# Hybrid mixer block on one core: splitting, transposing and gating the projection's results while it runs, memory tokens in plain fp32, half of a branch projection within retention

## The chip, the cores and the metric

The kernel runs on one core of one Trainium2 chip. The metric is the time of one execution in microseconds (us); of several runs the median is taken. The engines are TensorE (PE in the rows, with its weight loads as PEld), VectorE (DVE), ScalarE (ACT), GpSimd (POOL) and SyncE (SP), which issues nearly all DMAs here. TensorE's clock is granted at one of two levels, 1.2 and 2.4 GHz; the rows give the mean as a share of the higher one.

## The reference

One decoder layer over 1024 rows of 1024 features. `z` is 13312 columns wide and is cut into the operands of three branches and three gates.

```python
h = rms_norm(x, g_mix[l])
z = h @ w_in[l]
rq, rk, rv, rg, dq, dk, dv, cq, gates = split_cols(z, SPLITS)
ret = retention_chunkwise(rq, rk, rv)              # 4 heads, chunks of 128 rows
ret = jax.nn.swish(rg) * head_norm(ret, g_ret[l], True)
y_ret = ret @ w_ret_o[l]                           # 2048 -> 1024
da = diff_attention(dq, dk, dv, lam)               # 4 heads, causal, ALiBi
y_diff = head_norm(da, g_diff[l], False) * (1.0 - lam_init) @ w_diff_o[l]
kv = rms_norm(mem, g_mem[l]) @ w_mem_kv[l]         # 256 memory tokens
ca = memory_cross_attention(cq, mk, mv)
y_cross = ca.reshape(b, s, CROSS_W) @ w_cross_o[l]
g = jax.nn.sigmoid(gates)
merged = g[0] * y_ret + g[1] * y_diff + g[2] * y_cross
x = x + merged @ w_out[l]
u = jax.nn.relu(rms_norm(x, g_ffn[l]) @ w_up[l])
x = rms_norm(x + (u * u) @ w_down[l], g_final)
```

## The kernel before, in words

Features lie on the 128 partitions and rows of the sequence along the free axis, in two halves `t` of 512. Nearly every product is three matmuls (`mm3`, L144 to L146): each operand is split into a high and a low fp32r part, and high x high, high x low and low x high are added in PSUM. A split is a cast on ScalarE (L131) and a subtraction on VectorE (L132). The stages follow each other:

1. **Prologue.** `x` is normalized and made into the seven operands `hop` of a seven-product scheme. Beside that the keys and values of the memory tokens are computed (`mem_keys`, `mem_values`): 16 weight tiles `kst`, each split into `kw`, against the split memory `mh`, in 384 matmuls of 256 columns.
2. **Projection.** 52 units of 256 columns of `z` go through `seven`: seven `quad`s of twelve 512-column matmuls each, with the left operands (`wo`) made by ScalarE and VectorE one unit ahead. `z_emit` is called four times in a unit (tile `zo`): VectorE adds a PSUM tile and an earlier copy `s`, or ScalarE copies, and SP stores the fp32 tile to DRAM. The units run in the order cq, dq, dk, dv, rk, rq, rv, rg, gates.
3. **Cross-attention**, 4. **differential attention**: `load_halves` loads a tile of `z` (`raw`), and ScalarE and VectorE split it; `dv` is transposed on TensorE first (`dvt`). After every second block, `fill` puts one half tile of a branch's output projection (`branch_halves`, 24 matmuls `y`) between.
5. **Retention**, 32 steps (4 heads x 8 chunks). `ret_prepare` forms the scores from plain fp32 operands (`rsc`, L784), and transposes and splits v and k (`rvt`, `rkt`); `ret_product` multiplies and updates the state; `ret_store` transposes the result (`rot`) and stores it (`rn`). 16 `fill`s of the second branch's projection lie in every second step.
6. **Retention's output projection** (`branch`, w_ro in two halves of 8 features blocks): `make_ret` loads `rn` and `rg`, multiplies by the gate on ScalarE, VectorE and GpSimd, and splits (`ar`), twice; then 384 matmuls `y` each time.
7. Output projection (`wo`), MLP and the final norm.

Gates are loaded and put through a sigmoid beside each `y` tile (L454, L944). Instructions reach each engine's queue in an order that a scheduler fixes when the program is built; each engine then works through its own queue in that order.

Of the kernel before, what the change touches and what calls it, by code (L numbers as in the profile page):

```python
# [18 lines left out]
P = 128  # L19
# [16 lines left out]
FILL_R = [[1, 0] * 4] * 4  # L36
# [21 lines left out]
def hybrid_block(  # L58
# [57 lines left out]
    z_d = pairs("z", NU)  # L116
# [6 lines left out]
    def z_of(col, t):  # L123
        return z_d[INDEX[col]][t]

    def gate_of(n, t):
        return z_of(GT + (n // 2) * 256, t)[:, n % 2]
# [69 lines left out]
    def left_operands(pool, src0, src1):  # L197
# [10 lines left out]
        for key, src in (  # L208
            ("11", ra[:, 0]), ("12", ra[:, 1]), ("2", s2), ("1", s1), ("3", rb[:, 0]), ("22", rb[:, 1]), ("4", s4)
        ):  # L210
            w = pool.tile([P, 2, HALF], F32R, tag="wo", name="wo", bufs=12)
            split(w[:, 0], w[:, 1], src)
            ops[key] = w
# [16 lines left out]
    def seven(units, ops, load, tmp, emit):  # L230
# [3 lines left out]
        def begin(u):  # L234
# [3 lines left out]
            s1 = tmp.tile([P, HALF], F32, tag="s1", name="s1", bufs=2)  # L238
# [5 lines left out]
        for i, u in enumerate(units):  # L244
# [13 lines left out]
            s3 = tmp.tile([P, HALF], F32, tag="s3", name="s3", bufs=2)  # L258
# [17 lines left out]
    def kv_load(src):  # L276
        st = sp0.tile([P, 1024], F32, tag="kst", name="kst", bufs=3)
        nc.sync.dma_start(out=st, in_=src)
        return st

    def kv_split(st):
        w = sp0.tile([P, 2, 1024], F32R, tag="kw", name="kw", bufs=2)
        split(w[:, 0], w[:, 1], st)
        return w
# [6 lines left out]
    early = [kv_load(w_kv[f]) for f in range(2)]  # L291
# [24 lines left out]
    mh = [sp0.tile([P, 2, HALF], F32R, name=f"mh{j}", tag=f"mh{j}") for j in range(4)]  # L316

    def mem_hl(k):
        v = mh[k // 2]
        c = (k % 2) * NMEM  # L320
        return v[:, 0, c : c + NMEM], v[:, 1, c : c + NMEM]

    for j in range(4):
        r = sp0.tile([P, HALF], F32, tag="tt", name="mr", bufs=6)
        for k in (2 * j, 2 * j + 1):
            c = (k % 2) * NMEM
            src = mt[k // 4][:, (k % 4) * NMEM : (k % 4 + 1) * NMEM]
            scale_rows(r[:, c : c + NMEM], src, vec[:, V_MEM + k : V_MEM + k + 1], rb[:, :NMEM])
        split(mh[j][:, 0], mh[j][:, 1], r)
# [5 lines left out]
    def x_steps():  # L335
        for t in range(2):
            for acc in wide_sums([xr[kp][t].rearrange("p a c -> p (a c)") for kp in range(4)]):
                yield
            rb = rms_finish(acc, HALF)
            yield  # L340
            for kp in range(4):
                for a in range(2):
                    v = xr[kp][t][:, a]
                    k = 4 * a + kp
                    scale_rows(v, v, vec[:, V_MIX + k : V_MIX + k + 1], rb)
# [5 lines left out]
        for kp in range(4):  # L351
# [4 lines left out]
            add(b12, b22, b12, ALU.subtract)  # L356
            add(t4, b21, t2, ALU.subtract)
# [17 lines left out]
    def mem_keys(f):  # L375
        hl = kv_split(early[f] if f < 2 else kv_load(w_kv[f]))
        o = mm_ps("mk")
        for k in range(KT):
            sl = slice(k * P, (k + 1) * P)
            mm3(o[:, :NMEM], (hl[:, 0, sl], hl[:, 1, sl]), mem_hl(k), k == 0, k == KT - 1)  # L380
        kv_store(mk_d[f // 2][:, f % 2], o[:, :NMEM])

    def mem_values(h):
        hls = [kv_split(kv_load(w_kv[8 + 2 * h + j])) for j in range(2)]
        for m in range(2):
            o = mm_ps("mv")
            for k in range(KT):
                c = (k % 4) * 256
                w = hls[k // 4]
                a = tuple(v[:, m * P : (m + 1) * P] for v in mem_hl(k))  # L390
                mm3(o[:, :256], a, (w[:, 0, c : c + 256], w[:, 1, c : c + 256]), k == 0, k == KT - 1)
# [19 lines left out]
    def z_emit(u, n, t, a, b):  # L411
        st = zt.tile([P, HALF], F32, tag="zo", name="zo", bufs=4)
        if b is None:
# [3 lines left out]
        nc.sync.dma_start(out=z_d[u][t][:, n], in_=st)  # L417
# [28 lines left out]
    def branch_halves(b, w, w0, rhs, before):  # L446

        for d in range(8):
            hl = weight(w[w0 + d])
            for t in range(2):  # L450
# [3 lines left out]
                nc.scalar.activation(out=g, in_=g, func=AF.Sigmoid)  # L454
                add(g, o, g, ALU.mult)
                if before:
                    m = zs_tile("hf", "m")
                    nc.sync.dma_start(out=m, in_=mg_d[d][t])
                    nc.gpsimd.tensor_tensor(out=g, in0=g, in1=m, op=ALU.add)
                nc.sync.dma_start(out=mg_d[d][t], in_=g)  # L460
                yield

# [23 lines left out]
    def v_tile(name):  # L486
        return cp.tile([P, 2, 2, 256], F32R, tag="v", name=name, bufs=4)
# [673 lines left out]
```

## Time and profile before

| | us |
|---|---|
| median of 3 runs | 2768.16 (2762.69 to 2782.67) |
| the profiled execution | 2767.48 |
| its span | 2765.7 |
| PE busy | 2610.9 (94%) |
| DVE busy | 1567.6 (57%) |
| ACT busy | 998.0 (36%) |
| POOL busy | 127.2 (5%) |

The span is what the trace covers, and the profiled execution's own time is 1.8 us more. Busy shares are means over the stages listed above, which differ; a stage's share is read from its own stretch. The mean granted clock is 0.975 of the higher level. A matmul's row is longer than its distance to the next one, since matmuls are pipelined; the distance between starts is the price in a stream.

### The profile page before, as it was taken

To read this page: it belongs to the slowest core of one execution; us is meant where nothing else is said; L and a number is where in the kernel's file an instruction comes from. 1 tells how busy PE (TensorE), PEld (TensorE's weight loads), DVE (VectorE), ACT (ScalarE), POOL (GpSimd) and SP (SyncE) were. 2 spreads that over 40 slices of the span, in tenths; PEclk is the share of its full clock that TensorE was granted. 3 is DMA by queue.
4 is the path that set the end of the run, shared out by engine and by line. 5 is a ranking of instruction groups with operands and counts; after the bars stand their busy time and mean duration, and the time that the engine had idled before them with its cause. 6 is when DMAs were issued, how large, how long until landed. Compare 5 with 4: busy or idle time off the path is not lost. (4 is left out here: it accounts for less than half of the span.)

```text
span 2765.7 us, 32055 instructions
## 1 busy us (share of the span) xinstructions
PE 2610.9 (94%) x12126; PEld 2145.0 (78%) x12126; DVE 1567.6 (57%) x2749; ACT 998.0 (36%) x1803; POOL 127.2 (5%) x135
## 2 busy tenths in 40 slices
PE   6899999999999998799879998699999999999998
PEld 5788888888888887688767776477888888888887
DVE  7745454454544542877768787554564444544445
ACT  5433333333333332667665443332342112121222
POOL 0000000000000000000101111320000000000001
PEclk9999999999999999899989999699999999999999
DMA  5333332333333332423327443653321111111111
GB/s 201 135 111 110 114 112 103 111 108 114 114 103 111 107 107 88 157 92 127 121 92 252 159 156 127 212 179 102 123 88 54 46 46 46 46 56 52 46 38 61
DMA packets 135595, 299.15 MB, mean 108 GB/s; under 512 B 13712, under 2 KB 42384, under 8 KB 135440
## 3 DMA queue, kind: packets, MB, share of 16 engines
q1 hardware_dynamic: 135296, 297.06, 31.8%
q8 instruction: 95, 1.56, 0.2%
q14 instruction: 60, 0.49, 0.1%
q10 hardware_dynamic: 144, 0.03, 0.0%
HBM read 215.26 MB, written 81.79 MB: 107 GB/s over the span
## 5 line engine op out<-in xcount | busy, mean ns | idle before, releaser
L144 PE MATMUL x<-hop,wo 128*128 128x512 f32 x1456 | 575.1, 395 | 6.0 <-ACT wo L131 5.3
L146 PE MATMUL x<-hop,wo 128*128 128x512 f32 x1456 | 571.7, 393 | 0.0
L145 PE MATMUL x<-hop,wo 128*128 128x512 f32 x1456 | 566.1, 389 | 0.0
L146 PEld LDWEIGHTS x<-hop,wo 128*128 128x128 f32 x1456 | 274.0, 188 | 64.4 <-DVE wo L132 0.2
L144 PEld LDWEIGHTS x<-hop,wo 128*128 128x128 f32 x1456 | 274.4, 188 | 61.0 <-ACT wo L131 5.5
L145 PEld LDWEIGHTS x<-hop,wo 128*128 128x128 f32 x1456 | 274.0, 188 | 61.3
L132 DVE TENSOR_TENSOR wo<-wr,wo 128x512 fp32r<-128x512 f32 x208 | 143.7, 692 | 238.6 <-ACT wo L131 238.6
L149 DVE TENSOR_TENSOR zo<-x,s 128x512 f32<-128x512 f32 x156 | 107.9, 692 | 243.2 <-PE x L146 127.7
L131 ACT CAST whl<-wst 128x1024 fp32r<-128x1024 f32 x112 | 115.8, 1047 | 336.3 <-PE dn L146 257.3
L1040 DVE TENSOR_TENSOR x<-x,dn 128x512 f32<-128x512 f32 (+1 forms) x248 | 164.5, 669 | 128.0 <-PE dn L146 127.6
L145 PE MATMUL dn<-u,whl 128*128 128x512 f32 (+1 forms) x544 | 207.4, 381 | 0.0
L144 PE MATMUL dn<-u,whl 128*128 128x512 f32 (+1 forms) x544 | 206.4, 379 | 0.0
L146 PE MATMUL dn<-u,whl 128*128 128x512 f32 (+1 forms) x544 | 204.5, 376 | 0.0
L145 PE MATMUL u<-h,whl 128*128 128x512 f32 x512 | 200.4, 391 | 0.0
L144 PE MATMUL u<-h,whl 128*128 128x512 f32 x512 | 199.8, 390 | 0.0
L146 PE MATMUL u<-h,whl 128*128 128x512 f32 x512 | 199.6, 390 | 0.0
L131 ACT CAST wo<-wr 128x512 fp32r<-128x512 f32 x208 | 128.9, 622 | 165.6 <-PE x L146 161.9
L132 DVE TENSOR_TENSOR whl<-wst,whl 128x1024 fp32r<-128x1024 f32 x112 | 143.2, 1289 | 32.7 <-ACT whl L131 32.2
L1018 DVE TENSOR_TENSOR ur<-ur 128x512 f32<-128x512 f32 x64 | 44.3, 692 | 194.9 <-ACT ur L1017 194.9
L144 PE MATMUL y<-ar,whl 128*128 128x512 f32 x256 | 105.8, 416 | 35.5 <-ACT ar L131 35.5
L131 ACT CAST wo<-ws 128x512 fp32r<-128x512 f32 x156 | 96.8, 622 | 110.0 <-PE x L146 106.3
L132 DVE TENSOR_TENSOR wo<-ws,wo 128x512 fp32r<-128x512 f32 x156 | 107.2, 689 | 27.1 <-ACT wo L131 27.0
(243 smaller groups left out, 4680.0 us busy)
## 6 DMA issues: line engine op xcount, KB each, us to landing
wr<-in_w_z SPq DMA_DIRECT2D x104, 512.0 KB, 3.4
z<-zo SPq DMA_DIRECT2D x208, 256.0 KB, 2.0
g<-z SPq DMA_DIRECT2D x64, 256.0 KB, 3.4
wst<-in_w_up SPq DMA_DIRECT2D x32, 512.0 KB, 3.3
wst<-in_w_down SPq DMA_DIRECT2D x32, 512.0 KB, 3.3
raw<-z SPq DMA_DIRECT2D x24, 512.0 KB, 3.3
kst<-in_w_kv SPq DMA_DIRECT2D x16, 512.0 KB, 4.0
mg<-g SPq DMA_DIRECT2D x32, 256.0 KB, 2.0
```

What stands on the lines that cost most here:

```text
L131: nc.scalar.copy(out=hl_hi, in_=src)
L132: eng.tensor_tensor(out=hl_lo, in0=src, in1=hl_hi.bitcast(F32), op=ALU.subtract)
L144: nc.tensor.matmul(out, ah, bh, start=first, stop=False, skip_group_check=again)
L145: nc.tensor.matmul(out, ah, bl, start=False, stop=False, skip_group_check=again)
L146: nc.tensor.matmul(out, al, bh, start=False, stop=last, skip_group_check=again)
L149: nc.vector.tensor_tensor(out=out, in0=a, in1=b, op=op)
L1018: nc.vector.tensor_tensor(out=r, in0=r, in1=r, op=ALU.mult)
L1040: nc.vector.tensor_tensor(out=x2[d][t][:, cols], in0=x2[d][t][:, cols], in1=o[:, :width], op=ALU.add)
```

## The change

The splits, transposes and gates that stages 3 to 6 did after loading `z` are done in `z_emit`, before the store. Query and key tiles are stored as split pairs (`zh`, 512 KB instead of 256 KB for a tile); k and v of retention and v of the differential branch are transposed there (four 128x128 transposes, tile `zt`, for each of the 64 tiles of 16 units) and stored split (`zth`, also in tag `zh`, two buffers). `rg` becomes swish times the gain, the gates become sigmoids. The later stages load them ready. Retention's scores take the split pairs, as six fp32r matmuls of 128 columns instead of two plain fp32 ones. In the prologue the memory products are 128 plain fp32 matmuls, without splits; half of the scaling of `x` and two of its four subtractions go to ScalarE and GpSimd. `FILL_R` puts a half tile into every retention step: first the 16 of w_do, then from step h = 2, c = 1 the first half of w_ro, whose features are by then stored. The second half of w_ro runs after retention. GpSimd's add in `branch_halves` goes to VectorE, and two scalings of results (`don`, `on`) go from VectorE to ScalarE.

```diff
-FILL_R = [[1, 0] * 4] * 4
+FILL_R = [[1] * 8] * 4
...
     def mem_keys(f):
-        hl = kv_split(early[f] if f < 2 else kv_load(w_kv[f]))
+        w = early[f] if f < 4 else kv_load(w_kv[f])
         o = mm_ps("mk")
         for k in range(KT):
-            sl = slice(k * P, (k + 1) * P)
-            mm3(o[:, :NMEM], (hl[:, 0, sl], hl[:, 1, sl]), mem_hl(k), k == 0, k == KT - 1)
+            nc.tensor.matmul(
+                o[:, :NMEM], w[:, k * P : (k + 1) * P], mem_of(k), start=k == 0, stop=k == KT - 1
+            )
...
     def z_emit(u, n, t, a, b):
+        col = ORDER[u]
         st = zt.tile([P, HALF], F32, tag="zo", name="zo", bufs=4)
+        if col >= GT:
+            if b is not None:
+                add(st, a, b)
+            nc.scalar.activation(out=st, in_=a if b is None else st, func=AF.Sigmoid)
+            nc.sync.dma_start(out=z_d[col][t][:, n], in_=st)
+            return
         if b is None:
             nc.scalar.copy(out=st, in_=a)
         else:
             add(st, a, b)
-        nc.sync.dma_start(out=z_d[u][t][:, n], in_=st)
...
+        if col in zh_d:
+            zh = zt.tile([P, 2, HALF], F32R, tag="zh", name="zh", bufs=2)
...
+                split(zh[:, 0], zh[:, 1], st)
+            nc.sync.dma_start(out=zh_d[col][t][:, :, n], in_=zh.bitcast(F32))
+        if col in zt_d:
+            tp = sc_ps("zt")
+            for i in range(4):
+                nc.tensor.transpose(out=tp[:, i * P : (i + 1) * P], in_=st[:, i * P : (i + 1) * P], identity=ident)
+            zh = zt.tile([P, 2, HALF], F32R, tag="zh", name="zth", bufs=2)
...
+                split(zh[:, 0], zh[:, 1], tp)
+            nc.sync.dma_start(
+                out=zt_d[col][t][:, :, :, n * P : (n + 1) * P],
+                in_=zh.rearrange("p a (i c) -> p a i c", i=4).bitcast(F32),
+            )
...
     def cross_probs(h, mk, t):
-        q = load_halves(qk_tile("q", "cq"), z_of(CQ + h * 256, t))
+        q = load(qk_tile("q", "cq"), zh_d[CQ + h * 256][t])
...
-    def ret_prepare(h, c, kqv):
...
+    def ret_prepare(h, c, kq):
...
         for d in range(2):
-            nc.tensor.matmul(sp[:, :P], kc[:, d], qc[:, d], start=d == 0, stop=d == 1)
+            mm3(sp[:, :P], (k[:, 0, d, sl], k[:, 1, d, sl]), (q[:, 0, d, sl], q[:, 1, d, sl]), d == 0, d == 1)
...
+        vhl = rp.tile([P, 2, HALF], F32R, tag="vhl", name="vhl", bufs=3)
+        for b in range(2):
+            nc.sync.dma_start(
+                out=vhl[:, :, b * 256 : (b + 1) * 256].bitcast(F32), in_=zt_d[RV + h * 512 + b * 256][t][:, :, i]
+            )
...
+            if h == 2 and c == 1:
+                drain()
+                ar = [[None] * 2 for _ in range(KT)]
+                for t in range(2):
+                    ret_features(0, 4, t)
+                halves = branch_halves(0, w_ro, 0, hl_rhs(ar), True)
             fill(FILL_R[h][c])
...
+    for t in range(2):
+        ret_features(4, 8, t)
+    halves = branch_halves(0, w_ro, 8, hl_rhs(ar), True, out=mg)
+    drain()
...
-    branch(2, 0, w_ro, 0, make_ret(0))
-    branch(3, 0, w_ro, 8, make_ret(4))
```

`ret_features`, new, loads a stored feature tile into `arr` (tag `hf`, two buffers of the pool) and splits it into `ar`, whose memory is that of the operand tiles of the branch projected before.

TensorE's queue in the projection, at the seam between one unit's last product (`x3`) and the next unit's first (`x2`), in a unit of dv. Before:

```order
L145 MATMUL x3_3044<-hop_1001,wo_2874 128x512
L146 MATMUL x3_3044<-hop_1001,wo_2874 128x512
L144 MATMUL x2_3151<-hop_430,wo_2996 128x512
L145 MATMUL x2_3151<-hop_430,wo_2996 128x512
L146 MATMUL x2_3151<-hop_430,wo_2996 128x512
```

The same seam now:

```order
L156 MATMUL x3_3133<-hop_705,wo_2923 128x512
L154 MATMUL x2_3264<-hop_374,wo_3077 128x512
L155 MATMUL x2_3264<-hop_374,wo_3077 128x512
L156 MATMUL x2_3264<-hop_374,wo_3077 128x512
L154 MATMUL x2_3264<-hop_395,wo_3077 128x512
L449 MATMUL zt_3223<-ident_68,zo_3221 128x128 x4
L155 MATMUL x2_3264<-hop_395,wo_3077 128x512
```

The transposes of a tile stand four matmuls (elsewhere seven) behind the product that it came from, in the middle of the next one.

ScalarE's queue over most of one unit of rk (`s` are the copies that free `x1` for TensorE's next product, `wo` the operands of the next unit). Before:

```order
L131 CAST wo<-ws 128x512 [waits DVE_49,PE_49]
L254 COPY s_3453<-x_3348 128x512 [waits PE_49]
L131 CAST wo<-wr 128x512 [waits DMAHW7_49]
L131 CAST wo<-wr 128x512 [waits PE_49]
L259 COPY s_3480<-x_3348 128x512 [waits PE_49]
L131 CAST wo<-ws 128x512 [waits DVE_49,Activation_49]
L239 COPY s_3498<-x_3485 128x512 [waits PE_49]
L131 CAST wo<-ws 128x512 [waits Activation_49]
L414 COPY zo<-x_3348 128x512 [waits DMAHW7_49,PE_49,Activation_49]
```

Now:

```order
L141 CAST zh<-zo 128x512 [waits DMAHW5_49,DVE_49]
L141 CAST wo<-wr 128x512 [waits PE_49]
L145 ACTIVATE zth<-zt,vec 128x512 [waits DMAHW7_49,DVE_49]
L269 COPY s_3701<-x_3533 128x512 [waits PE_49]
L141 CAST wo<-wr 128x512
L141 CAST zh<-zo 128x512 [waits DMAHW0_49,DVE_49]
L249 COPY s_3731<-x_3718 128x512 [waits PE_49]
L141 CAST wo<-ws 128x512
L145 ACTIVATE zth<-zt,vec 128x512 [waits DMAHW1_49,Activation_49]
L427 COPY zo<-x_3533 128x512 [waits PE_49]
```

Each `zh` and `zth` waits for a DMA, that of the tile that had the buffer, and the `s` copies stand behind them.

TensorE's queue where retention ends (`rot` are the last transposes of its results). Before:

```order
L146 MATMUL ro_14852<-Shl_14796,qhl_14770 128x512
L867 MATMUL rot_14873<-ident_68,on_14808 128x128 x4
L867 MATMUL rot_14882<-ident_68,on_14871 128x128 x4
L144 MATMUL y_15073<-ar_14936,whl_15070 128x512
L145 MATMUL y_15073<-ar_14936,whl_15070 128x512
```

Now:

```order
L156 MATMUL y_15727<-ar3_1_0_14293,whl_15724 128x512
L893 MATMUL rot_15759<-ident_68,on_15708 128x128 x4
L154 MATMUL y_15771<-ar0_0_1_14298,whl_15724 128x512
L155 MATMUL y_15771<-ar0_0_1_14298,whl_15724 128x512
L156 MATMUL y_15771<-ar0_0_1_14298,whl_15724 128x512
```

Two half tiles of the first half of w_ro (`y_15727` before the last `rot`, `y_15771` after it, 24 matmuls each) now stand where the first `y` of w_ro stood.

## Rows read from the trace of the kernel before

**Rows 1.** Windows by stage: length, busy us (instructions) by engine, clock, DMA share, GB/s.

```profile
0.00:95.50 95.50, 62.16 (x411) 57.74 (x411) 75.12 (x116) 50.98 (x77) 3.43 (x9) 0.94 0.51 178
95.50:1099.20 1003.70, 1003.03 (x4368) 822.14 (x4368) 491.88 (x727) 325.55 (x571) 0.00 (x0) 1.00 0.31 108
1099.20:1174.70 75.50, 53.56 (x327) 45.85 (x327) 59.99 (x122) 50.99 (x116) 0.00 (x0) 0.88 0.51 173
1174.70:1452.50 277.80, 248.33 (x1406) 205.61 (x1404) 201.16 (x590) 182.28 (x391) 26.73 (x32) 0.96 0.33 108
1452.50:1720.00 267.50, 249.84 (x1253) 203.29 (x1254) 217.33 (x465) 121.47 (x248) 38.40 (x48) 0.97 0.52 169
1720.00:1952.00 232.00, 193.47 (x772) 151.17 (x773) 119.00 (x155) 80.04 (x127) 46.23 (x32) 0.88 0.50 164
1952.00:2765.70 813.70, 800.47 (x3596) 659.24 (x3594) 403.16 (x577) 186.70 (x275) 12.44 (x14) 0.99 0.18 58
```

**Rows 2.** Timeline of PE at the stages' seams: start, length, group [idle before, releaser].

```profile
17.00 0.79 PE L144 MATMUL mk<-mh,kw 128*128 128x256 f32 x2 [1.62 <-ACT mh L131]
...
95.47 0.80 PE L144 MATMUL x<-hop,wo 128*128 128x512 f32 x1 [5.29 <-ACT wo L131]
...
1112.40 0.58 PE L144 MATMUL csc<-mk,cq 128*128 128x256 f32 x1 [13.13 <-ACT cq L131]
```

**Rows 3.** Timeline of PE in one retention step, in a stream.

```profile
1686.24 0.60 PE L867 MATMUL rot<-ident,on 128*128 128x128 f32 x4
1686.67 0.61 PE L784 MATMUL rsc<-rq,rk 128*128 128x128 f32 x4
1687.12 0.60 PE L791 MATMUL rvt<-ident,rvr 128*128 128x128 f32 x4
1687.56 0.38 PE L798 MATMUL rkt<-ident,rk 128*128 128x128 f32 x2
1687.69 0.47 PE L144 MATMUL ro<-vhl,shl 128*128 128x512 f32 x1
```

**Rows 4.** Timeline of PE in the prologue: fp32r matmuls of 256 columns.

```profile
23.13 0.28 PE L146 MATMUL mk<-mh,kw 128*128 128x256 f32 x1
23.25 0.28 PE L144 MATMUL mk<-mh,kw 128*128 128x256 f32 x1
```

**Rows 5.** The page's groups: a split of 512 columns on ScalarE and VectorE.

```profile
L131 ACT CAST wo<-wr 128x512 fp32r<-128x512 f32 x208 | 128.9, 622 | 165.6 <-PE x L146 161.9
L132 DVE TENSOR_TENSOR wo<-wr,wo 128x512 fp32r<-128x512 f32 x208 | 143.7, 692 | 238.6 <-ACT wo L131 238.6
```

**Rows 6.** DMA issues: KB of one, median us from issue to landing.

```profile
wr<-in_w_z SPq DMA_DIRECT2D x104, 512.0 KB, 3.4
...
rvr<-z SPq DMA_DIRECT2D x16, 512.0 KB, 5.1
...
rq<-z SPq DMA_DIRECT2D x8, 512.0 KB, 5.8
```

**Rows 7.** Waits of PE from 1175 to 1460 us: total, times, longest.

```profile
PE dtp L683 <- DVE ds L672: 8.3, 7, 2.2
PE dot L718 <- DVE don L712: 6.4, 12, 2.0
PE rsc L784 <- DMA rq<-z: 5.9, 1, 5.9
```

**Rows 8.** Groups of ScalarE: loads of function tables for sigmoid (L454) and exponential (L662).

```profile
L454 ACT ACT_TABLE_LOAD x16 | 20.5, 1283 | 0.8 <-DMA g<-z 0.5
L662 ACT ACT_TABLE_LOAD x14 | 18.0, 1283 | 4.2 <-DVE dnm L656 4.0
```

**Rows 9.** Timeline of PE after retention, then its waits from 1720 to 1910 us.

```profile
1731.02 0.79 PE L144 MATMUL y<-ar,whl 128*128 128x512 f32 x1 [10.02 <-ACT ar L131]
...
1738.14 0.79 PE L144 MATMUL y<-ar,whl 128*128 128x512 f32 x1 [3.49 <-ACT ar L131]
...
PE y L144 <- ACT ar L131: 35.5, 9, 10.0
```

More of the change, by code (lines that the diff above doesn't have):

```diff
@@ L114, in pairs, with scratch @@
         return [[dram.tile([P, 2, HALF], F32, name=f"{name}{i}_{t}", tag=f"{name}{i}_{t}") for t in range(2)] for i in range(n)]
-    z_d = pairs("z", NU)
+    def scratch(name, shape):
+        return [dram.tile(shape, F32, name=f"{name}_{t}", tag=f"{name}_{t}") for t in range(2)]
+    z_d, zh_d, zt_d = {}, {}, {}
+    for col in ORDER:
+        if col >= GT or RG <= col < DQ:
+            z_d[col] = scratch(f"z{col}", [P, 2, HALF])
+            continue
+        if RV <= col < RG or DV <= col < CQ or RK <= col < RV:
+            zt_d[col] = scratch(f"zt{col}", [P, 2, 4, 256])
+        if not (RV <= col < RG or DV <= col < CQ):
+            zh_d[col] = scratch(f"zh{col}", [P, 2, 2, HALF])
     da_d = pairs("da", NH)
@@ L290, in hybrid_block @@
         mt.append(m)
[L291 removed]
+    early = [kv_load(w_kv[f]) for f in range(4)]
     xr = [[None] * 2 for _ in range(4)]
@@ L339, in x_steps @@
             rb = rms_finish(acc, HALF)
+            row = sp0.tile([P, HALF], F32, tag="row", name="row", bufs=1)
+            nc.scalar.copy(out=row, in_=rb)
             yield
@@ L387, in mem_values @@
             for k in range(KT):
[L388 to L391, printed above, removed]
+                nc.tensor.matmul(
+                    o[:, :256],
+                    mem_of(k)[:, m * P : (m + 1) * P],
+                    ws[k // 4][:, (k % 4) * 256 : (k % 4 + 1) * 256],
+                    start=k == 0,
+                    stop=k == KT - 1,
+                )
             kv_store(mv_d[h][:, m], o[:, :256])
@@ L458, in branch_halves, with hl_rhs @@
                     nc.sync.dma_start(out=m, in_=mg_d[d][t])
-                    nc.gpsimd.tensor_tensor(out=g, in0=g, in1=m, op=ALU.add)
-                nc.sync.dma_start(out=mg_d[d][t], in_=g)
+                add(g, o, g, ALU.mult)
+                if out is not None:
+                    add(out[d][t], g, m)
+                else:
+                    if before:
+                        add(g, g, m)
+                    nc.sync.dma_start(out=mg_d[d][t], in_=g)
                 yield
+    def hl_rhs(ops):
+        return lambda k, t: (ops[k][t][:, 0], ops[k][t][:, 1])
     halves = iter(())
@@ L868, in ret_store @@
         st = zs_tile("sp", "spill", 3)
-        nc.scalar.copy(out=st, in_=tp)
         t, off = c // 4, (c % 4) * P
+        sg = rp.tile([P, 4, P], F32, tag="sg", name="sg", bufs=2)
+        for b in range(2):
+            nc.sync.dma_start(out=sg[:, 2 * b : 2 * b + 2], in_=z_d[RG + h * 512 + b * 256][t][:, :, off : off + P])
+        add(st, tp, sg.rearrange("p f c -> p (f c)"), ALU.mult)
         for e in range(2):
@@ L875, in ret_store, with ret_features @@
             )
-    halves = branch_halves(1, w_do, 0, lambda k, t: (ad[k][t][:, 0], ad[k][t][:, 1]), True)
+    def ret_features(j0, j1, t):
+        for j in range(j0, j1):
+            for e in range(2):
+                raw = zs_tile("hf", "arr")
+                nc.sync.dma_start(out=raw, in_=rn_d[j][t][:, e])
+                k = 2 * j + e - (2 * j0 // 8) * 8
+                ar[k][t] = bp.tile([P, 2, HALF], F32R, name=f"ar{j}_{e}_{t}", tag=f"b{k}_{t}")
+                split(ar[k][t][:, 0], ar[k][t][:, 1], raw)
+    halves = branch_halves(1, w_do, 0, hl_rhs(ad), True)
     done = None
```

209 lines of the change are left out of this document (70 added, 139 removed).

## The prediction

> **What bounds the kernel now.** I read the windows by stage first [rows 1], since a mean over the span hides that the stages differ. In the projection TensorE is busy 1003.03 of 1003.70 us at the full clock while ScalarE and VectorE use a third and a half of it: there only TensorE's own instructions count, and 1003.7 us over 4368 matmuls is 0.23 us for each of 512 columns. In the last window (output projection, MLP) it is 98%. Everywhere else TensorE has holes: 62.2 of 95.5 us busy in the prologue, where VectorE is busy 75.1; 53.6 of 75.5 at a mean clock of 0.88 in cross-attention; 193.5 of 232.0, also at 0.88, in retention's output projection. What ends these holes stands in the timeline and the waits: casts on ScalarE behind a DMA or behind other casts [rows 2, 9], VectorE's softmax work [rows 7]. The change thus moves work from engines that TensorE waits for into the stage in which they are idle; but it moves 256 transposes there too, and these are TensorE's own. I price each stage by counts of TensorE's instructions and add the waits that stay.
>
> **Prices in a stream.** From the distances of starts in one retention step [rows 3]: four 128x128 transposes take 0.43 to 0.45 us, so 0.11 each; two plain fp32 matmuls of 128 columns take 0.45, so 0.225 each. A plain one of 256 columns is then 0.45; an fp32r one of 256 columns takes 0.12 [rows 4].
>
> **Prologue.** Removed are all splits of the memory weights, which VectorE and ScalarE did between the steps for x, and a part of the x work goes to GpSimd, which is idle there (3.4 us busy) [rows 1]. TensorE gets slower work: 128 plain matmuls x 0.45 = 57.6 us, where three of 0.12 would be 0.36 each, 46 in all. With VectorE relieved by half, TensorE becomes the bound. It started on the keys at 17.0 us [rows 2]; I take 15, since two splits went ahead of it. To the 57.6 I add 8 us, an estimate for the low clock at the start and the sums for the norms that stand in its queue. The last product ends at 80.6; from there to the projection's first matmul I keep the 5.5 us of before (95.47 less the end of the products, of which 5.29 us were idle [rows 2]), since the load of the first weights again stands behind the last store on SP. That gives 86.1 instead of 95.5: **-9.4**. Bounds: -14 if the 8 us are half as many; the other end is a rival below.
>
> **Projection.** Added: 64 tiles x four transposes x 0.11 = 28.2 us, wholly on the path, as nothing in this stage hides TensorE's work. They wait for VectorE's add: 0.2 us from the product's end, 0.69 for the add, which is close to the four matmuls (0.92 us) in front of them in the queue. I take 0.1 us of stall for each tile, 6 us (bounds 0 and 20, 0.3 each). A third term is the ring of two `zh` buffers. One pass through a buffer is a cast 0.62, a subtraction 0.69 [rows 5], some 0.5 for handshakes and the issue on SP, and the landing of 512 KB, 3.4 us in this stage [rows 6]: 5.2 us. A unit of rk uses eight such tiles, so two buffers need 4 x 5.2 = 20.8 us, and the unit itself lasts 84 x 0.23 + 16 x 0.11 = 21.1. It just fits. The emits come in bunches, though (three within 5.5 us), and a cast that waits for its buffer holds back ScalarE's `s` copies behind it, for which TensorE waits. I take 5 us for the four units of rk (bounds 0 and 29). The units of dq, dk, dv, rv, rq and cq use four tiles and are safe. Sigmoids and the gains for rg are hidden: ScalarE has two thirds of the stage free. DMA traffic in a unit of rk rises to 5 MB in 21 us, 240 GB/s, where 108 GB/s made a share of 0.31 [rows 1], so about 0.7. Sum: 28.2 + 6 + 5 = **+39**.
>
> **Cross-attention and differential attention.** In cross, the first score waited 13.1 us for the cast of cq [rows 2], whose load waited for `raw` buffers. Now it is loaded ready. I take **-6** for the start and the ScalarE work of the eight tiles (bounds -10 and 0). In differential attention 64 transposes go, 7 us. The waits for the softmax [rows 7] should shrink, since the 30 table loads of 1.28 us between sigmoid and exponential [rows 8], the splits of q, k and v and one scaling leave the two engines: of some 23 us of such waits, of which the two longest groups are shown, and of the low clock behind them I take 11. Against that stands that k's first half of the next head, read until the last block, is now a 1 MB load where a `raw` tile lay ready: three seams, 1 us each. Sum **-15** (bounds -28 and +3). The start of retention, 5.9 us behind the load of rq [rows 7], waits for twice the bytes: **+2**.
>
> **From retention to the output projection.** Before, 1452.5 to 1952.0, 499.5 us [rows 1]. TensorE's work in it: 432 products of retention and 1152 of `y`, 1584 x 0.23 = 364.3; `rsc` 64 x 0.225 = 14.4; 312 transposes 34.3. Together 413.0, so 86 us are lost, 35.5 of them in waits for `ar` alone [rows 9]. After: the same 364.3; `rot` 14.1; and the scores, now 192 fp32r matmuls of 128 columns. The trace has none. Bounds: 0.12, the price of twice the columns [rows 4], and 0.225, that of a plain matmul of this shape in this place [rows 3]. I take the upper one, because that row is the only one with tiles of 128 columns, and because the kernel itself widens a score of 128 columns to 256 (`wide` in `diff_scores`), which would make no sense if narrow ones ran at streaming price: 192 x 0.225 = 43.2. Work: 421.6. For the losses I go through the queue. Every step now has 24 `y` matmuls behind the `rot`, so the chain from scores to `shl` and from state to `Shl` is covered; I take 10 us over 32 steps and the loads of `ad`. At h = 2, c = 1 and again after retention 16 feature tiles pass two `hf` buffers, a load of some 3.3 us and a split for each pair, about 2.3 us a tile, against 0.69 us of products that each tile allows. At the first place two retention steps and a last `y` cover it (8 us lost); at the second only `y_15771` and the interleaved tiles do (15). For `am`, which now lies in the memory of `ar`, 2.5, and 5 for changes of tile shape. Sum 40.5, so 462.1: **-37.4** (bounds -66, with cheap scores and fewer losses, and -15).
>
> Here a rule of the Trainium skill speaks against my price: "TensorE: Matmul & The Clock Gate", section "Back-to-back issue gap", gives about 81 ns for each 128-column matmul in a stream, and makes no exception for fp32r. No row here shows such a tile. By that figure the scores would take 192 x 0.081 = 15.6 us, 27.6 less than in my sum, which would then give 2713; the next section works the same case out from the rows alone.
>
> **Sum.** -9.4 + 39 - 6 - 15 + 2 - 37.4 = -26.8. From the profiled execution's 2767.5 this gives 2740.7; the median of the runs is 0.7 higher, so I say **2741**, 1.0% less. What a measurement of this kernel can tell from no change is about 1%, 28 us.
>
> **Rivals.**
> *Narrow fp32r runs at streaming price.* At 0.12 the scores take 23.0 us, 20.2 less: 2721. For it: 256 columns do stream at 0.12, half of 512. Against it: the widened scores.
> *The zh ring is too slow, and the kernel ends slower than before.* With a landing of L us, two buffers need 4 x (1.8 + L) for a unit of rk against 21.1. At 5.8, as retention's loads of the same size take at a DMA share of 0.52 [rows 6, 1], the four units lose 4 x (30.4 - 21.1) = 37 instead of 5: 2773. It decides from L = 5.5, where the 26.8 won are gone. For it: share 0.7 in these units. Against: `wr`, beside which these stores run, lands in 3.4, and loads in bursts are what made 5.8.
> *Filling retention gives nothing back.* A step now moves about 2.8 MB (v, k, q, gates, results, weights, `m`) in 10.5 us, 270 GB/s, where 169 GB/s made a share of 0.52 [rows 1]: 0.83. If loads come late and a step takes 11.6 us, 32 x 1.1 = 35 are lost: 2776.
> *Plain fp32 does not hold the clock up.* At the low level the 128 matmuls take 0.9 each, 57.6 more: 2798.
>
> **How the numbers follow.** My forecast 0.42, cheap scores 0.25, zh ring 0.13, starved retention 0.12, low clock 0.05, something else 0.03. The range takes the first two with their bounds (2741 less 20 for the scores and 24 for attention, prologue and losses that turn out best) and the middle of the next two with 10 us more: 2697 to 2786. Faster by over 1% (under 2740.5): half of the forecast, nine tenths of the cheap scores, 0.45; slower by over 1% (over 2796): 0.09; within: 0.46.
>
> **What would show it.** The projection's window should last 1036 to 1050 us, with the `zt` transposes at 0.11 and PE's waits for `zo` at 0.1 us each; waits of `zh` for a DMA in the rk units tell of the ring. The first x matmul should stand at 86 us, with a granted clock near 1 from 25 us on. The distance of starts of `rsc` gives the disputed price. There should be one or two table loads in cross and differential attention together. After the last `rot` TensorE should wait some 10 us in all, not 35. I am wrong if TensorE has many short waits in the projection, which would turn its 39 us into 70, or if the steps of retention are longer than 11 us.

## The result and the profile after

The changed kernel takes 2737.98 us, median of 4 runs (2736.15 to 2745.52); the kernel before took 2765.93 beside it. The ratio is 0.9892, with the 95% interval 0.9847 to 0.9937: some 1.1% less, where 2741 and 1.0% were forecast. The profiled execution, the longest of the four, took 2745.5; its span is 2743.7, 22.0 less than before.

The sum of the prediction can be held against the trace stage by stage. The seams are the first x matmul, the end of the last one, the first retention score and the first `wo`.

| stage | before | after | difference | predicted |
|---|---|---|---|---|
| prologue | 95.5 | 90.1 | -5.4 | -9.4 |
| projection | 1003.7 | 1038.1 | +34.4 | +39 |
| cross and differential attention | 353.3 | 318.8 | -34.5 | -19 |
| retention to output projection | 499.5 | 482.3 | -17.2 | -37.4 |
| the rest | 813.7 | 814.4 | +0.7 | 0 |
| sum | 2765.7 | 2743.7 | -22.0 | -26.8 |

The whole came out as forecast, but that is luck: attention won 15 us more than was said and the projection lost 5 less, retention won 20 less and the prologue 4 less, and these cancel. The table's windows of the kernel after (attention in one; retention cut at its last `rot`) in the columns of [rows 1]:

```profile
0.00:90.10 90.10, 66.94 (x282) 54.82 (x282) 57.65 (x79) 39.85 (x67) 27.72 (x25) 0.97 0.53 188
90.10:1128.20 1038.10, 1035.38 (x4624) 842.03 (x4624) 604.90 (x903) 454.87 (x783) 0.00 (x0) 1.00 0.45 145
1128.20:1447.00 318.80, 285.66 (x1667) 241.46 (x1666) 213.73 (x639) 168.10 (x454) 25.50 (x32) 0.97 0.54 192
1447.00:1819.50 372.50, 332.38 (x1500) 264.09 (x1501) 219.66 (x476) 102.67 (x167) 19.21 (x32) 0.95 0.81 257
1819.50:1929.30 109.80, 103.94 (x406) 78.56 (x406) 43.10 (x59) 20.83 (x29) 0.00 (x0) 0.91 0.51 166
1929.30:2743.70 814.40, 800.22 (x3595) 658.74 (x3593) 411.86 (x591) 192.67 (x286) 12.47 (x14) 1.00 0.18 59
```

The projection is still TensorE's alone (1035.4 of 1038.1). In retention VectorE is busy 219.7 of 372.5 us, a share of 0.59 where it was 0.81 (217.33 of 267.5) [rows 1]; new is a DMA share of 0.81 there, where it was 0.52.

The seams in PE's timeline, against [rows 2]:

```profile
13.67 12.83 PE L381 MATMUL mk<-mh,kst 128*128 128x256 f32 x46 [0.57 <-DVE mh L197]
...
71.16 3.72 PE L391 MATMUL mv<-kst,mh 128*128 128x256 f32 x16 [1.51 <-ACT kvs L374]
...
90.15 0.79 PE L154 MATMUL x<-hop,wo 128*128 128x512 f32 x1 [5.38 <-ACT wo L141]
...
1138.94 0.55 PE L154 MATMUL csc<-mk,cq 128*128 128x256 f32 x1 [10.58 <-DMA cq<-zh]
...
1447.02 0.47 PE L154 MATMUL rsc<-rq,rk 128*128 128x128 f32 x1 [8.63 <-DMA rq<-zh]
```

In the projection the transposes stand between x matmuls:

```profile
365.33 0.60 PE L449 MATMUL zt<-ident,zo 128*128 128x128 f32 x4
365.68 0.48 PE L155 MATMUL x<-hop,wo 128*128 128x512 f32 x1
...
371.83 0.66 PE L449 MATMUL zt<-ident,zo 128*128 128x128 f32 x4
372.24 0.48 PE L155 MATMUL x<-hop,wo 128*128 128x512 f32 x1
```

Four take 0.35 to 0.41 us to the next start, a little under the 0.43 to 0.45 priced. In retention, the six scores of a step in a stream:

```profile
1779.82 0.22 PE L154 MATMUL rsc<-rq,rk 128*128 128x128 f32 x1
1779.88 0.27 PE L155 MATMUL rsc<-rq,rk 128*128 128x128 f32 x1
1779.99 0.28 PE L156 MATMUL rsc<-rq,rk 128*128 128x128 f32 x1
1780.10 0.27 PE L154 MATMUL rsc<-rq,rk 128*128 128x128 f32 x1
```

The starts are 0.11 us apart. A narrow fp32r tile costs half of what the plain one of [rows 3] does, so that 192 scores take 21 us, not 43. The rule of the Trainium skill ("TensorE: Matmul & The Clock Gate", "Back-to-back issue gap", about 81 ns) is nearer than my 0.225, but the measured 110 ns decide.

Where retention lost time stands in TensorE's waits from the first score to `wo`, and in VectorE's from there to the last `rot` (total, times, longest):

```profile
PE rst L154 <- DVE sf L816: 18.2, 11, 3.8
PE y L154 <- ACT ar L141: 11.3, 9, 2.6
...
PE y L154 <- ACT ad L141: 4.5, 7, 1.0
PE ro L154 <- DMA vhl<-zt: 3.8, 1, 3.8
PE ro L156 <- DVE shl L142: 3.8, 2, 3.5
PE ro L154 <- ACT shl L141: 1.8, 2, 1.1
PE y L155 <- DVE ar L142: 1.7, 4, 0.9
```

```profile
DVE g L159 <- DMA g<-z: 33.0, 14, 4.2
```

The features (`ar`) cost 13 us and not 35 [rows 9]; the longest item is one that the prediction did not have. TensorE's rows add up to 45 us. One wait of the longest item, in the timeline of all engines:

```profile
1603.01 0.61 SPq L495 DMA_DIRECT2D g<-z  x1
...
1604.59 2.58 SPq L901 DMA_DIRECT2D rn<-spill  x2
...
1609.13 0.69 DVE L159 TENSOR_TENSOR g<-y,g 128x512 f32<-128x512 f32 x1 [3.35 <-DMA g<-z]
1609.85 0.69 DVE L159 TENSOR_TENSOR g<-g,m 128x512 f32<-128x512 f32 x1
1610.46 0.28 DVE L816 TENSOR_TENSOR sf<-rsc,masks 128x128 f32<-128x128 f32 x1
...
1610.80 0.80 PE L154 MATMUL rst<-vhl,khl 128*128 128x512 f32 x1 [3.65 <-DVE sf L816]
```

VectorE stands still until a gate has landed; its product starts 6.1 us after the load's issue. The mask of the next scores (`sf`) is queued behind that product, and TensorE waits for the bank that the mask empties. Before, a sigmoid on ScalarE stood between the load and the product. There ScalarE stopped for a gate's load, though once and not 14 times, and VectorE never did (it waited 6.3 us, twice, for the sigmoid):

```profile
ACT g L454 <- DMA g<-z: 6.4, 1, 6.4
```

ScalarE's table loads, against [rows 8], are down to two behind the start, one at the first gate of rg and one at the first exponential:

```profile
L432 ACT ACT_TABLE_LOAD x1 | 1.3, 1283 | 0.0
L580 ACT ACT_TABLE_LOAD x1 | 1.3, 1283 | 5.9 <-issue 5.9
```

### The profile page after: what moved, and what is told of

It is laid out like the page before. It is cut to its first block, busy times and chain, and to the rows that moved or that the text cites. A ratio compares the mean times of both kernels' runs of the same rounds, so it can differ in the third digit from the quotient of the medians.

```text
span 2743.7 us, 32286 instructions
## 1 busy us (share of the span) xinstructions
PE 2624.5 (96%) x12070; PEld 2139.7 (78%) x12070; DVE 1550.9 (57%) x2745; ACT 979.0 (36%) x1784; POOL 84.9 (3%) x103
## 4 chain that ended last, share of the span: by engine, by line
PE 56%; issue 27%; DMA 8%; DVE 6%; ACT 2%; SPq 1%; POOL 1%; POOLq 0%; DVEq 0%; ACTq 0%
PE x L154 12%; PE x L156 12%; PE x L155 12%; PE y L154 3%; PE y L156 3%; PE y L155 3%; DMA g<-z 2%; DMA adr<-da 2%; DMA arr<-rn 1%; PE wo L155 1%; PE wo L156 1%; PE zt L449 1%; PE wo L154 1%; DVE hop L142 1%; DVE g L159 1%
## 5 line engine op out<-in xcount | busy, mean ns | idle before, releaser
L142 DVE TENSOR_TENSOR whl<-wst,whl 128x1024 fp32r<-128x1024 f32 x112 | 135.4, 1220 | 26.7 <-ACT whl L141 26.6
L1009 ACT ACTIVATE ur<-u 128x512 f32<-128x512 f32 x64 | 38.2, 598 | 233.4 <-PE u L156 233.4
L159 DVE TENSOR_TENSOR g<-y,g 128x512 f32<-128x512 f32 x64 | 44.2, 690 | 133.3 <-PE y L156 80.3
```

Of the source, the lines that this page charges most:

```text
L142: eng.tensor_tensor(out=hl_lo, in0=src, in1=hl_hi.bitcast(F32), op=ALU.subtract)
L159: nc.vector.tensor_tensor(out=out, in0=a, in1=b, op=op)
L1009: nc.scalar.activation(out=r, in_=o, func=AF.Relu)
```

## The experiments

Twelve kernels ran, each an edit of the changed kernel. The stages are in us from the same seams, with attention cut at `lps`, a small product at the end of cross-attention (82.4 and 271.0 before); the ratio is to the kernel before, with its interval.

| kernel | median | ratio | prologue | projection | cross | diff | retention to `wo` |
|---|---|---|---|---|---|---|---|
| changed | 2737.98 | 0.9892 (0.9847, 0.9937) | 90.1 | 1038.1 | 69.5 | 249.3 | 482.3 |
| e1 spills' own buffers | 2716.48 | 0.9837 (0.9818, 0.9856) | 89.1 | 1036.1 | 68.4 | 248.5 | 453.7 |
| e2 no fill with w_ro | 2745.80 | 0.9939 (0.9918, 0.9959) | 90.5 | 1037.9 | 69.9 | 250.5 | 487.2 |
| e3 merged DMAs | 2742.25 | 0.9925 (0.9902, 0.9948) | 90.2 | 1037.1 | 69.0 | 248.1 | 482.0 |
| e4 sigmoid in diff | 2756.02 | 0.9972 (0.9959, 0.9985) | 88.7 | 1036.6 | 67.6 | 266.5 | 478.4 |
| e5 e1 and more loads moved | 2711.26 | 0.9793 (0.9756, 0.9829) | 85.3 | 1037.2 | 68.7 | 247.7 | 458.9 |
| e6 split memory | 2754.05 | 0.9948 (0.9921, 0.9975) | 101.2 | 1040.6 | 68.9 | 252.6 | 472.8 |
| e7 one zh buffer | 2800.52 (1 run) | | 89.3 | 1100.2 | 68.1 | 252.2 | 474.6 |
| e8 wide scores | 2721.35 | 0.9827 (0.9782, 0.9871) | 89.7 | 1036.0 | 68.1 | 249.7 | 460.4 |
| e9 e1, stores on ScalarE | 2714.71 | 0.9819 (0.9793, 0.9845) | 87.7 | 1037.3 | 68.4 | 250.3 | 454.2 |
| e10 e9, wide scores | 2714.15 | 0.9813 (0.9788, 0.9838) | 84.9 | 1037.1 | 70.0 | 249.7 | 458.2 |
| e11 e9, raw tiles, x on VectorE | 2701.37 | 0.9776 (0.9751, 0.9800) | 78.7 | 1037.7 | 69.7 | 251.2 | 451.1 |
| e12 e1 without the fill | 2739.77 | 0.9909 (0.9880, 0.9937) | 90.0 | 1037.4 | 70.5 | 247.9 | 476.9 |

In e4, e6 and e7 the SP queue of retention holds the same entries in the same order as in the changed kernel; the four stretches, 472.8 to 482.3, show what executions alone differ by there.

**e1: the spills' own buffers.**

```diff
-        st = zs_tile("sp", "spill", 3)
+        st = rp.tile([P, HALF], F32, tag="spl", name="spill", bufs=3)
```

> The spilled results of retention get three buffers of their own, so that the gate loads have the old ring of three to themselves; nothing else changes. Theory 'late gate': in the changed kernel the load of a gate stands on SP behind the stores of a retention step because it waits for one of the three buffers that both share; VectorE then stops at the product with the gate, the mask of the scores stands behind it, and TensorE waits for the scores' bank (five waits of 2.1 to 3.8 us, 15 in all, with some 2 us of low clock behind each). Then these waits go and the stretch from the first score of retention to w_out falls from 482 to about 460 us, the time from 2738 to about 2716. Rival 'bandwidth': the loads are late because the DMA engines are 0.84 busy there; then an earlier issue lands no earlier, at most 5 us are won (2733 or more).

Retention fell to 453.7, under all four of those stretches, the time to 2716. Waits of VectorE and TensorE in retention:

```profile
DVE g L159 <- DMA g<-z: 2.6, 3, 1.5
```

```profile
PE rst L154 <- DVE sf L816: 5.0, 4, 2.1
```

VectorE's waits for gates fell from 33.0 to 2.6 us and TensorE's for the bank from 18.2 to 5.0. The DMA share from the first score to `wo` is 0.78 where it was 0.74, and a gate lands 4.4 us after its issue where it took 4.6 (medians), so bandwidth was not what made the gates late. They are issued earlier: in the median some 20 us before their half tile's products end, where it was 5. Nothing was edited but the buffers, but with them SP's queue came out in another order; whether the load waits for a buffer of the ring or for its place in an order that the ring forces, this run does not tell apart.

By the runs the gain over the changed kernel is smaller than by the stage, and the intervals of the two ratios just overlap (0.9837 against 0.9892). They lie well apart from e3, timed beside e1 (0.9925), in which retention takes what it takes in the changed kernel.

**e2: the fill undone.**

```diff
-FILL_R = [[1] * 8] * 4
+FILL_R = [[1, 0] * 4] * 4
...
-            if h == 2 and c == 1:
-                drain()
...
+    for t in range(2):
+        ret_features(0, 4, t)
+    halves = branch_halves(0, w_ro, 0, hl_rhs(ar), True)
+    drain()
```

> The part on w_ro alone is undone: the first half of w_ro runs after retention again, and the fill is one half tile in every second step. The half tiles of w_ro then no longer cover the steps, and the loads and splits of 32 feature tiles instead of 16 stand in front of products with nothing else to do. Theory 'the fill is worth something': the stretch from the first score to w_out grows from 482 to about 495 us, 2751 in all. Rival 'starved retention': half as many gate, sum and weight loads during retention make its steps faster by what the feature waits cost, the stretch stays within 5 us of 482 (2738).

487.2, between the two: 5 us over the changed kernel, 9 to 14 over three executions with its order. In the changed kernel the fill was worth little. VectorE's waits for gates, with half as many gates in retention, as before the change:

```profile
DVE g L159 <- DMA g<-z: 14.8, 5, 3.9
```

The late gates do not come from the fill alone.

**e3: one DMA instead of two.**

```diff
-        for b in range(2):
-            nc.sync.dma_start(
-                out=vhl[:, :, b * 256 : (b + 1) * 256].bitcast(F32), in_=zt_d[RV + h * 512 + b * 256][t][:, :, i]
-            )
+        nc.sync.dma_start(out=vhl.bitcast(F32), in_=rv_d[h][t][:, :, i])
...
```

> The buffers in DRAM of v, of the gates and of the results of a retention head are one tensor for each half of the sequence, so that a step issues one DMA instead of two for each of v, the gate and the results: 8 issues a step where there were 11, the same bytes, v in pieces of 2 KB instead of 1 KB. Rival 'SP issues': SP issues for 202 of 340 us in retention, in order; with 3 x 0.6 us less a step, the gate loads go out earlier and 10 to 15 us are won (2723 to 2728). Theory 'late gate' (a ring of three buffers that the gates share with the spills): the loads still wait for the buffer, at most 5 us (2733 to 2738).

482.0: three issues less a step won nothing, and VectorE still waits 26.2 us for gates, where it was 33.0. The number of issues on SP is not the cause.

**e4: one sigmoid back in differential attention.**

```diff
+            if col < GT + 2048:
                 nc.scalar.activation(out=st, in_=a if b is None else st, func=AF.Sigmoid)
...
+                if b == 2:
+                    nc.scalar.activation(out=g, in_=g, func=AF.Sigmoid)
```

> The gates of the cross branch alone (8 of 24 blocks) are stored raw by the projection, and their sigmoid is applied where the product is made, within differential attention, as in the kernel before. Theory 'table loads': the switches between sigmoid and exponential on ScalarE, some 30 of 1.28 us, are the larger part of the 22 us that differential attention won; then it grows from 249 to about 262 us or more (2751 or more). Rival 'transposes and splits': the 64 transposes of v and the splits of q, k and v are what was won; then the stretch grows by less than 4 us (2738 to 2742).

Differential attention took 266.5 instead of 249.3 us. ScalarE's groups show that the loads of the tables are back, while transposes and splits are as in the changed kernel:

```profile
L500 ACT ACT_TABLE_LOAD x15 | 19.2, 1283 | 1.7 <-DMA g<-z 1.4
L701 ACT ACT_TABLE_LOAD x14 | 18.0, 1283 | 0.2
```

Of the 22 us that this stage won, 17 came back with 29 loads, 37 us of ScalarE, and the 16 sigmoids that call for them; the run does not tell the loads from the sigmoids. TensorE's waits in the stage, 22.9 us before and 9.5 in the changed kernel, are 20.0 here.

**e5: more loads out of each other's way.** On top of e1:

```diff
-        nc.sync.dma_start(out=dst, in_=st)
+        nc.scalar.dma_start(out=dst, in_=st)
...
-                raw = zs_tile("hf", "arr")
+                raw = pool.tile([P, HALF], F32, tag="raws", name="arr", bufs=3)
...
+            ret_inputs(h, (1,), kqv)
```

> On top of the spills' own buffers: the raw tiles of the features of both branches get three buffers of their own instead of the two that they share with the merged sums; the second halves of k and q of the first retention head are loaded after the first chunk's values and the first features, not before; the stores of the memory keys and values go out on ScalarE's queue, so that the projection's first weight load no longer stands behind the last of them on SP. Theory 'loads behind other loads': the 11 us of waits for the features fall to about 5, the 3.8 us for the first v go, the first x matmul comes up to 4 us earlier: 10 to 15 us less than with the spills' buffers alone, about 2704. Rival 'bandwidth': the loads are late because the engines are busy; then at most 4 us are won (2712 or more).

2711, 5 us less than e1: just past the rival's 4 us and far from the theory's 10 to 15. The store on ScalarE's queue brought the first x matmul to 85.3, 4 us before e1's. The later loads of k and q won nothing: the first score still waited 9.0 us for `rq`, 8.6 in the changed kernel, so the loads behind it had not held it up. The 3.8 us for the first v went, but a wait of 8.1 us for `shl` came, and retention was 5 us longer than in e1.

**e6: the memory tokens split as before**, `mem_keys` and `mem_values` as in the kernel before, the other edits of the prologue kept.

```diff
-        w = early[f] if f < 4 else kv_load(w_kv[f])
+        hl = kv_split(early[f] if f < 2 else kv_load(w_kv[f]))
...
+            mm3(o[:, :NMEM], (hl[:, 0, sl], hl[:, 1, sl]), mem_hl(k), k == 0, k == KT - 1)
```

> The memory tokens alone are as before, split into two fp32r halves with three products of each; the rest of the changed kernel stays, the x work on GpSimd too. Theory 'splits on VectorE': they were what bounded the prologue, the 5.3 us that it won go back: first x matmul at 95 us, 2743. Rival 'GpSimd': what was won came from the adds and scalings moved to GpSimd; then the first x matmul comes at 92 us or less.

Both were wrong: 101.2, 11.1 us more than in the changed kernel and 5.7 more than before the change. The plain fp32 products won about twice what the stage shows, and something else in the prologue lost a part of it: e11.

**e7: one zh buffer.**

```diff
-            zh = zt.tile([P, 2, HALF], F32R, tag="zh", name="zh", bufs=2)
+            zh = zt.tile([P, 2, HALF], F32R, tag="zh", name="zh", bufs=1)
```

> One zh buffer instead of two for the split and transposed results in the projection, nothing else. If a pass through a buffer takes 5.2 us, as the prediction worked out, the eight tiles of a unit of rk take 42 us where the unit lasts 21, which costs 4 x 21 = 84 us, and the units with four tiles, 21 us in one buffer, lose about a microsecond each: the projection grows from 1038 to 1120 to 1150 us. If the ring had much slack, with a pass of 3 us, the rk units lose 4 x 3 = 12 us and the others nothing: 1050 us.

1100.2: 62 us more than with two, under the range of the first and far over the second. By the starts of every 84th `x` matmul, the eight units of rk and rq take 212 us instead of 165 and those of rv 12 us more; the loss of rk comes only with the units behind it. In these 212 us 48 tiles pass the buffer, so that a pass takes at most 4.4 us, an estimate, instead of 5.2. ScalarE's longest waits of that kernel for the buffers:

```profile
ACT zh L141 <- DMA zh<-zh: 45.2, 29, 3.8
ACT zth L145 <- DMA zh<-zh: 32.3, 15, 3.9
ACT zth L141 <- DMA zt<-zth: 27.6, 26, 2.5
```

All such waits are 146 us here and 28 in the changed kernel, where TensorE's in the whole projection are 7.6 us, of which 5.4 stand before its first matmul. One buffer is too few for this stage, and two were enough.

**e8: wide scores.**

```diff
-            mm3(sp[:, :P], (k[:, 0, d, sl], k[:, 1, d, sl]), (q[:, 0, d, sl], q[:, 1, d, sl]), d == 0, d == 1)
+            mm3(sp[:, :256], (k[:, 0, d, sl], k[:, 1, d, sl]), (q[:, 0, d, wd], q[:, 1, d, wd]), d == 0, d == 1)
```

> The scores of retention are computed 256 columns wide, of which the 128 that are needed are used: twice the columns, the same 192 matmuls. If a narrow fp32r tile costs as much as a wide one (0.11 against 0.12 us in the rows), the stretch from the first score to w_out grows by some 2 us and the time stays at 2738. Rival 'price by columns': at 0.11 for 128 columns it is 0.22 for 256, 21 us more, 2759.

The price came out as the first had it, 0.11 to 0.12 us for twice the columns:

```profile
1604.16 0.28 PE L154 MATMUL rsc<-rq,rk 128*128 128x256 f32 x1
1604.28 0.27 PE L155 MATMUL rsc<-rq,rk 128*128 128x256 f32 x1
1604.39 0.28 PE L156 MATMUL rsc<-rq,rk 128*128 128x256 f32 x1
```

The time did not: 2721, and retention took 460.4, which neither theory has. The scheduler had put SP's queue in another order there, and VectorE's waits for gates were 18.6 us instead of 33.0. e10, below, tests whether that is all.

**e9 and e10: the stores on ScalarE's queue, and wide scores on top.** The edits are those shown.

> The spills' own buffers, and the stores of the memory keys and values on ScalarE's queue; the loads of k and q of the first retention head and the features' raw tiles are as in the changed kernel. The prologue keeps the 4 us that the other queue won (first x matmul at 85 to 86 us), retention is that of the spills' buffers alone (454 us, up to 5 more or less by run): 2712.

> The same as the kernel with the spills' buffers and the stores on ScalarE's queue, with the scores of retention 256 columns wide. Theory 'order': the wide scores alone won 22 us in retention only because the order of SP's and VectorE's queues came out otherwise, with the gate loads in other places (VectorE's waits for them fell from 33 to 19 us); with the gates free of the spills' ring there is nothing left to win that way, and retention takes 450 to 460 us (2712). Rival 'wide scores are better in themselves': the 22 us come on top, retention falls under 440 us (2692).

2714.71 and 2714.15, retention 454.2 and 458.2: with the gates out of the spills' ring, wide scores win nothing. So what e8 won was not the tiles but, as far as the waits tell, the order around the gate loads. The first `x` matmul of e9 came at 87.7, later than said; e5 and e10, with the same prologue, have 85.3 and 84.9.

**e11: x on VectorE again, and raw tiles with buffers of their own**, on top of e9.

```diff
-                    scale_rows(v, v, vec[:, V_MIX + k : V_MIX + k + 1], rb, row if a == 1 else None)
+                    scale_rows(v, v, vec[:, V_MIX + k : V_MIX + k + 1], rb)
...
-            nc.gpsimd.tensor_tensor(out=b12, in0=b22, in1=b12, op=ALU.subtract)
-            nc.gpsimd.tensor_tensor(out=t4, in0=b21, in1=t2, op=ALU.subtract)
+            add(b12, b22, b12, ALU.subtract)
+            add(t4, b21, t2, ALU.subtract)
```

> Two edits in two stages, on top of the spills' buffers and the stores on ScalarE's queue. In the prologue all work on x is on VectorE again (the scalings of the second half of the rows, two of four sums of each operand group), as in the kernel before. Theory 'GpSimd holds VectorE up': while GpSimd works on two inputs in SBUF, VectorE's sums and differences of 512 columns take 1.7 us instead of 0.68; without it the first x matmul comes at 83 us or earlier. Rival 'VectorE is the bound': it comes later than 88 us. In retention and behind it the raw tiles of the features have three buffers of their own: the waits of TensorE for features, 15 us in all, fall to 8 or less, and the stretch from the first score to w_out to 448 us, or stays at 454 if these loads are late for want of bandwidth.

The first x matmul came at 78.7, the earliest of all. Groups of the prologue, first of the changed kernel (VectorE twice, GpSimd, ScalarE's casts twice), then of this one:

```profile
L142 DVE TENSOR_TENSOR hop<-xr,hop 128x512 fp32r<-128x512 f32 x16 | 18.3, 1182 | 0.0
...
L197 DVE SCALAR_TENSOR_TENSOR xr<-xr,vec,rb 128x512 f32<-128x512 f32 x8 | 5.5, 741 | 3.2 <-ACT row L341 3.2
```

```profile
L200 POOL TENSOR_TENSOR xr<-xr,row 128x512 f32<-128x512 f32 x8 | 11.3, 1440 | 6.2 <-ACT row L341 6.2
```

```profile
L141 ACT CAST hop<-xr 128x512 fp32r<-128x512 f32 x16 | 9.6, 618 | 9.9 <-POOL xr L200 4.8 <-POOL xr L358 3.6 <-DVE xr L197 1.5
L141 ACT CAST hop<-tt 128x512 fp32r<-128x512 f32 x12 | 7.3, 618 | 9.3 <-POOL tt L359 6.5 <-DVE hop L142 1.8 <-DVE tt L159 1.1
```

```profile
L142 DVE TENSOR_TENSOR hop<-xr,hop 128x512 fp32r<-128x512 f32 x16 | 10.6, 684 | 0.0
```

The 1182 ns are a mean: eight of the 16 subtractions ran beside GpSimd and took 1.69 us, eight ran without it and took 0.68, as all do in this run (684). A scaling that reads `rb` from PSUM takes 741 with GpSimd at work, as before the change (742). ScalarE's casts wait 14.9 us for GpSimd's own results, and the copies `kvs` stand in the same queue behind them. PE's timeline shows what follows: the last stretch of `mv` runs through, where the changed kernel stops three times for `kvs` (71.16 above is one). The edit also takes eight scalings and two copies (`row`) from ScalarE; how the gain divides between VectorE's slower sums, GpSimd's late results and this work, no run shows.

```profile
59.69 17.43 PE L389 MATMUL mv<-kst,mh 128*128 128x256 f32 x80
78.67 0.50 PE L154 MATMUL x<-hop,wo 128*128 128x512 f32 x1 [1.55 <-ACT wo L141]
```

From the first score to `wo` the features' waits, `ar` and `ad` together, fell from 17.6 us in e9 to 9.3 (8 were expected), and the stretch from 454.2 to 451.1, between the two figures expected and within what executions differ by. This version, 2701, beats both kernels.

**e12: the spills' own buffers without the fill.**

> The spills' own buffers, and the fill undone: the first half of w_ro after retention, one half tile in every second step. Theory 'the ring ate the fill': with the ring of three the fill was worth 5 us (487 less 482); with the ring free it is worth 12 to 20, so that this stretch takes 466 to 474 us where the filled one takes 454. Rival 'the fill is worth 5 us in any case, as the half tiles only move': 456 to 461 us.

476.9 against 453.7 with the fill: 23 us, more than the theory's 12 to 20. Half of w_ro within retention is worth that when the gates come in time. Against e2 the spills' buffers won 10 us without the fill, where they won 19 to 29 with it.

## Why the prediction came out as it did

The total was met because errors of the stages cancelled, as the table shows. The mechanism held in the projection; the prologue, the attention stages and retention each had a term that was wrong.

**Prologue**, -9.4 said, -5.4 measured. The first part was right: TensorE starts at 13.67 (15 was said), and its products run at the price taken (80 records, two to a product, in 17.43 us in the row of e11: 0.44 each). The products end at 84.8 and not at 80.6, with 4.0 us of waits for `kvs`, so TensorE was not the only bound. The step that failed is "a part of the x work goes to GpSimd, which is idle there", taken as relief for VectorE: VectorE's adds and differences beside GpSimd take 1.7 us instead of 0.68, ScalarE waits for GpSimd's results with TensorE's `kvs` behind them, and without the move the stage is 6 to 9 us shorter (78.7 against 84.9 to 87.7).

**Projection**, +39 said, +34.4 measured, inside the 1036 to 1050 named. A unit with four tiles takes 21.3 us instead of 19.2, by the starts of every 84th `x` matmul, so 0.53 for each tile: 0.39 from its first transpose to the next `x`, 0.14 beside. Over 64 tiles these are 25 and 9 us, where 28 and 6 were said. Of the ring's 5 us some 3 came, in two units of rk that take 23.1 and 22.0. e7 shows that the ring was no idle worry: with one buffer it costs 62 us.

**Cross and differential attention**, -19 with the start of retention, -34.5 measured. Cross won 12.9 where 6 were said, and only 2.5 of it at the wait for the first cq (13.1 to 10.6 us); the rest came behind the first score. Differential attention up to the first score of retention won 21.7 where 13 were said. The cover was named rightly, the table loads (30 before, one in these stages now), but the 11 us taken for the waits and the low clock behind them were too few: the waits alone fell by 13.4 us (22.9 to 9.5), and e4 gives the loads and the sigmoids together 17 us of differential attention.

**From retention to the output projection**, -37.4 said, -17.2 measured. Two errors of opposite sign stand in this term. The price of the scores, 0.225, was the wrong end: 0.11 is measured, 22 us less. The widened score in `diff_scores`, from which I argued, spoke rightly of the price for a column (256 cost as much as 128), but not for the tile. The losses were 40.5 in the sum; with 364 for products, 14 for `rot` and 21 for scores, 399 of work leave 83, of which 45 are the waits shown. What failed is "Every step now has 24 `y` matmuls behind the `rot`, so the chain from scores to `shl` and from state to `Shl` is covered; I take 10 us over 32 steps and the loads of `ad`": the waits for `sf`, `shl`, `vhl` and `ad` are 32 us, 18 of them for `sf`. This cover has a load of its own, the gate, which shares three buffers with the spills, and the chain's first step on VectorE is queued behind the product with it. The change took the sigmoid from ScalarE, the engine that used to wait for this load. That this move alone brought the wait to VectorE is argued from the traces; no run put the sigmoid back into retention. The features, for which I had taken 23 us, cost 13. For the 5 us of changes of tile shape the trace shows nothing: behind a score the next 512-column product starts 0.11 us later in the median, and behind such a product the score 0.24. The prediction named a sign for its own failure, steps of retention longer than 11 us, and it came true: 371.8 us for 32 steps are 11.6 each. e1 shows the late gates to be the cause, e3 speaks against the number of issues; starved retention, the rival that took just these 11.6 us, named the right place and the wrong reason, since e1 wins its 19 to 29 us at no lower a DMA share.

Left open is how much of the 38 us of losses that are no waits is due to the lower clock behind each wait; the windows show 0.95 and 0.91, and e1 has 0.96 from its first score to `wo`. Why retention varies by 10 us between executions with one order was not tried.

## What to carry to other kernels

When an operation is removed from an engine, ask which wait it used to take up, and on which queue that wait lands next; here VectorE, with the critical mask behind it, came to wait for a load for which ScalarE had waited before. Work put into gaps brings its own loads with it, and their buffers must not be shared with what they are to cover. A move to an idle engine is to be priced with what it does to the engine it relieves and to those that wait for its results. And a total that is met says little of the stages: compare them one by one.

## What was not expected of the hardware

An fp32r matmul of 128 columns costs 0.11 us in a stream, one of 256 columns 0.11 to 0.12 (e8): the second 128 columns cost next to nothing.

While GpSimd runs sums of two SBUF tiles, VectorE's operations with two SBUF inputs take up to 1.7 us instead of 0.68, and those with one input in PSUM are not slowed. The Trainium skill, "GPSIMD Engine Reference", section "1. Specifications", names this contention for VectorE instructions with two SBUF inputs; the trace agrees, with 1182 against 684 ns on average over 16 subtractions, of which eight ran beside GpSimd and took 1.69 us.

From the first score to `wo`, at a DMA share of 0.74 to 0.76, four executions with the same order of SP's queue differ by 10 us in 480, while the projection, at 0.45, stays within 5 us in 1038 over twelve kernels (all but e7).
